# Query and gate projections placed between the convolution blocks of a two-layer hybrid block, with convolution taps read from PSUM

## The chip, the cores and the metric

One core of a Trainium2 chip runs the whole program in one launch. The metric is device time in microseconds, the median of three runs. All times below are microseconds (us) unless marked ns. TensorE is called PE in the rows, VectorE DVE, ScalarE ACT, GpSimd POOL, and SyncE SP, which issues most DMAs.

## What is computed

Two layers of a diffusion backbone over 512 latent tokens (width 1024) and 256 context tokens. The reference, cut to what matters here:

```python
mod = (jax.nn.silu(c) @ mod_w[i] + mod_b[i])           # 6 vectors of 1024, for x and for ctx
h = rms_norm(x, norm_attn_w[i]) * (1.0 + sc_m) + sh_m   # the same for the context
ua, ub, ug = jnp.split(h @ w_in[i], splits, axis=-1)
ya, yca = neighbourhood_attention(ua, uca, na_rpb[i], ctx_out)
yb, ycb = ssd_mixer(ub, ucb, ssd_conv_w[i], ssd_conv_b[i], ...)   # z, xbc, dt; xbc = silu(conv5(xbc))
yg, ycg = gqa_attention(ug, ucg, q_norm_w[i], k_norm_w[i], ctx_out)
x = x + g_m * (jnp.concatenate([ya, yb, yg], axis=-1) @ w_out[i])
x = x + g_f * swiglu(hf, ffn_w_gate[i], ffn_w_up[i], ffn_w_down[i])
```

The second layer gives no context output, so its queries, gates and last two convolution blocks cover 512 tokens and not 768.

## The kernel before, in words

Each fp32 product is made of three fp32r matmuls, from a high and a low half of the weights and of the activations. `load_w` (L321) loads a weight block into one of two raw buffers `wr`, lets ACT write the high half (L326) into one of three buffers `wh`, and DVE subtract to get the low half (L327) into one of three `wl`. `proj_ws` (L338) keeps weights stationary and makes 128 output channels for all tokens in a two-bank PSUM tile `S` (two of them). `proj_as` (L352) keeps 128 tokens stationary and makes 256 or 272 output channels in a one-bank tile, `PT` or `sm` (two of each).

A layer runs: norm 1; query, key and value projections of the neighbourhood attention (`wblk(0)` to `wblk(5)`); `p_kv` (six token blocks, keys, values and dt of the other attention and of the SSD); `p_q` (L711, six token blocks, four in the second layer); eight blocks of `p_xbc` (L749); `p_z` twice (L798, six or four token blocks each); then the attention and SSD units, the output projection, norm 2 and the FFN.

`p_xbc` makes one block of 128 channels: 48 matmuls into `S`; ACT copies the two token ranges into `MA` with zero columns between (L758, L761), after which `S` is free; DVE makes tap 0 and the bias (L763) and taps 1 to 4 (L768) in `MB`; ACT takes the tanh (L772); DVE multiplies (L774, L776); for the first six blocks PE transposes six 128x128 pieces (L785) and ACT copies them out (L791). Beside blocks 0 to 2, `head_out` normalises and rotates key and query heads on POOL (L667, L673) and DVE (L683 to L688); beside blocks 1 to 3 `head_tr` transposes them (L695) and spills them (L282, L283).

The modulation of layer 0 is in twelve chunks of 512 columns. Chunks 0 to 3 are made on PE at the start (`mod_chunk`: eight matmuls at L178, two DVE copies at L185, four small matmuls at L188). Chunks 4 to 9 are made aside by `mod_dots`, each of 16 products on POOL (L228) and 16 sums on ACT (L229) over quarter-megabyte pieces in four `QN` buffers; SP issues those loads (L221) on the same queue as the weight loads (L323). `step_md` calls spread them over the projections and convolution blocks.

The order in each engine's queue is not the order of the text alone. A scheduler goes through all instructions with simulated times, and takes on each engine the first ready one in order of the text, so an engine can be given a later instruction early. The queues that it writes are then run in order on the chip.

Of the kernel before, what the change touches and what calls it, by code (L numbers as in the profile page):

```python
# [28 lines left out]
def hybrid_kernel(ctx: ExitStack, tc: tile.TileContext, a, out, dbg=None):  # L29
# [55 lines left out]
    class Split:  # L85
        """columns 0 .. 511 in one bank of PSUM, the others in another"""
# [12 lines left out]
    WB = {"wr": 2, "wh": 3, "wl": 3}  # L99
# [7 lines left out]
    # ---------------------------------------------------------- constants  # L107
# [42 lines left out]
    # ---------------------------------------------------------- modulation  # L150
# [8 lines left out]
    def mod_loads(l, c, tags):  # L159
        """512 columns of the modulation weights in tiles of the given tags, one or two k per tile"""  # L160
        w, k = [], 0
        for tag in tags:
            if tag in WB:
                wt, n = T(sb, tag, WB[tag], [P, 2, 512]), 2
            else:
                wt, n = T(sb, tag, BUFS[tag], [P, 1, 512]), 1
# [6 lines left out]
    def mod_chunk(l, c, w):  # L173
        """columns 512 c .. 512 c + 511 of the modulation; four row groups of the array take four k"""
# [21 lines left out]
    def mod_rows():  # L196
        """silu of both conditioning vectors as rows on every partition, in four tiles (vector, half)"""
# [11 lines left out]
    def mod_dots(l, c, rows, ptile, aside):  # L209
        """the same columns as mod_chunk by products along rows of the transposed weights"""  # L210
# [50 lines left out]
    # ---------------------------------------------------------- helpers  # L261
# [29 lines left out]
    def spread(rstd, n):  # L291
        """per-token values as a row on every partition"""
# [10 lines left out]
    def make_h(l, xT, h, pbs, part, shi, sc):  # L303
        """norm, scale and shift of one part of the tokens"""
# [16 lines left out]
    def load_w(src, n):  # L321
        raw = T(sb, "wr", 2, [P, n])
        nc.sync.dma_start(raw, src)  # L323
        hi = T(sb, "wh", 3, [P, n], F32R)
        lo = T(sb, "wl", 3, [P, n], F32R)
# [4 lines left out]
    def proj_ws(pt, wh, wl, xh, xl, nk, segs, ks=None):  # L330
        """pt[:, seg] = W^T x, W stationary (nk blocks of 128 rows)"""
# [13 lines left out]
    def proj_as(pt, ws, n, kper, xh, xl, t):  # L345
        """pt[:, :n] = x[t]^T W, activations stationary"""
# [28 lines left out]
    def attn(V2, xk, kts, qcols, bias, yout):  # L375
        """two heads and two blocks of queries; xk: range of x keys (or None); kts: key tiles for P V.
        Returns the steps of the four units: scores and softmax, transposes, and P V where one is complete"""
# [70 lines left out]
    # ---------------------------------------------------------- initial load and transpose  # L448
# [44 lines left out]
    for l in range(L):  # L493
# [9 lines left out]
        # ------------------------------------------------------ norm 1  # L503
# [6 lines left out]
        # ------------------------------------------------------ NA projections  # L510
# [3 lines left out]
        def spill(pt, n, name, scale, perm):  # L514
# [4 lines left out]
            if perm:  # L519
# [564 lines left out]
        for n, _ in enumerate(z for g in range(2) for z in p_z(g)):  # L1084
            if n == 2 * ntt - 2:
                scores(0)
# [284 lines left out]
```

## Time and profile before

| | us |
|---|---|
| runs of the kernel before | 1844.61, 1846.43, 1844.29 (median 1844.61) |
| span of the profiled execution, first to last instruction | 1843.3 |
| PE busy in the span | 1737.0 |
| DVE busy | 1104.0 |
| ACT busy | 681.5 |
| POOL busy | 423.1 |

No separate time is given for the profiled execution; its span is 1.3 below the median of the runs. Busy shares are averages over stages with different limits, so the rows further down are taken by stage: 62.4 to 121.5 (key, value and `p_kv` projections of layer 0), 121.5 to 301.6 (`p_q`, `p_xbc` and `p_z` of layer 0), 301.6 to 475 (its attention units), and 1182.6 to 1291 (`p_q`, `p_xbc` and `p_z` of layer 1). PEclk is the granted clock of TensorE, 1.00 being the upper of its two levels, 2.4 GHz, the lower being 1.2 GHz.

### The profile page before, as it was taken

What the parts mean: (1) busy time and instruction counts of PE and PEld (TensorE: products, weight loads), DVE (VectorE), ACT (ScalarE), POOL (GpSimd) and SP (SyncE); (2) the same over time, 40 slices, a digit from 0 to 9 for tenths busy, and PEclk for the clock granted to TensorE, in tenths of its full rate; (3) what the DMA queues carried; (4) which work ended last, traced back from release to release, by engine and by line L of the source; (5) the groups of instructions that cost most, each with busy time, mean ns of one, the idle gap of its engine ahead of it and who ended that gap; (6) DMA issues with size and microseconds to landing.
All of it is one profiled execution on the core that took longest, in us unless ns stands there. A gap on an engine that the chain in (4) does not pass through costs nothing.

```text
span 1843.3 us, 26677 instructions
## 1 busy us (share of the span) xinstructions
PE 1737.0 (94%) x10146; PEld 1478.4 (80%) x10146; DVE 1104.0 (60%) x2209; ACT 681.5 (37%) x1386; POOL 423.1 (23%) x429
## 2 busy tenths in 40 slices
PE   7987778989999999999999999999899999999998
PEld 3887667777878888888888887989677788888887
DVE  4559996877475555455654576587786743333334
ACT  5554555556344221121112224334555442232222
POOL 0488886654010000000000002241653100000000
PEclk9998889989989999999999999999999999999999
DMA  9542526433123334333443454342631323333332
GB/s 368 201 139 103 163 89 186 140 90 106 56 75 115 114 115 126 103 116 107 124 129 102 130 163 139 96 131 79 183 105 53 108 90 93 99 96 92 103 100 83
DMA packets 94319, 221.66 MB, mean 120 GB/s; under 512 B 18416, under 2 KB 26224, under 8 KB 94192
## 3 DMA queue, kind: packets, MB, share of 16 engines
q1 hardware_dynamic: 78096, 204.65, 35.6%
q10 hardware_dynamic: 16096, 15.31, 2.5%
q8 instruction: 80, 1.31, 0.3%
q14 instruction: 47, 0.39, 0.1%
HBM read 198.49 MB, written 21.43 MB: 119 GB/s over the span
## 4 chain that ended last, share of the span: by engine, by line
PE 76%; DVE 11%; DMA 5%; ACT 3%; issue 2%; POOL 2%; SPq 0%; ACTq 0%; DVEq 0%; POOLq 0%
PE S L338 61%; PE sm L436 3%; DVE MB L768 2%; DMA wl<-crow 2%; PE PT L424 2%; DVE wl L327 1%; PE PT L338 1%; PE PT L352 1%; PE sm L352 1%; DMA wr<-in_mod_wT_dram 1%; DVE wh L892 1%; PE S L390 1%; ACT wh L326 1%; PE sm L913 1%; PE sm L914 1%
## 5 line engine op out<-in xcount | busy, mean ns | idle before, releaser
L326 ACT ACTIVATE wh<-wr 128x1024 fp32r<-128x1024 f32 (+3 forms) x214 | 207.6, 972 | 732.2 <-PE S L338 542.4
L327 DVE TENSOR_TENSOR wl<-wr,wh 128x1024 fp32r<-128x1024 f32 (+3 forms) x214 | 250.0, 1169 | 174.0 <-ACT wh L326 171.6
L269 POOL TENSOR_TENSOR tiny<-tiny,mhalf 128x2 f32<-128x2 f32 (+2 forms) x17 | 28.7, 1688 | 1067.5 <-DVE tiny L1160 1020.3
L338 PE MATMUL S<-HY,wh 128*128 128x512 f32 (+1 forms) x716 | 214.0, 357 | 5.9 <-ACT HY L318 4.1
L338 PE MATMUL S<-HY,wl 128*128 128x512 f32 (+1 forms) x716 | 214.5, 357 | 0.0
L338 PE MATMUL S<-HZ,wh 128*128 128x512 f32 (+1 forms) x716 | 212.8, 355 | 0.8 <-DVE HZ L319 0.8
L338 PE MATMUL S<-HS,wl 128*128 128x512 f32 (+1 forms) x716 | 213.1, 355 | 0.0
L338 PE MATMUL S<-HS,wh 128*128 128x512 f32 (+1 forms) x716 | 211.1, 353 | 0.0
L231 DVE CUSTOM_DVE_ANT_0 PT<-wr,XFB 128x512 f32<-128x512 f32 x112 | 75.5, 715 | 179.8 <-DMA wr<-in_mod_wT_dram 179.8
L338 PEld LDWEIGHTS S<-HY,wh 128*128 128x128 f32 x716 | 119.8, 192 | 27.2 <-ACT HY L318 4.4
L338 PEld LDWEIGHTS S<-HZ,wh 128*128 128x128 f32 x716 | 118.2, 191 | 21.7 <-DVE HZ L319 2.2
L338 PEld LDWEIGHTS S<-HS,wh 128*128 128x128 f32 x716 | 118.8, 191 | 20.2
L338 PEld LDWEIGHTS S<-HY,wl 128*128 128x128 f32 x716 | 118.8, 191 | 18.8
L338 PEld LDWEIGHTS S<-HS,wl 128*128 128x128 f32 x716 | 118.0, 190 | 18.6
L338 PE MATMUL S<-PHA,wh 128*128 128x512 f32 (+1 forms) x358 | 106.4, 355 | 0.0
L338 PE MATMUL S<-PHB,wh 128*128 128x512 f32 (+1 forms) x358 | 105.0, 351 | 0.0
L338 PE MATMUL S<-GX,wh 128*128 128x512 f32 (+1 forms) x400 | 97.2, 349 | 0.4 <-DVE KA L1114 0.4
L415 POOL TENSOR_SCALAR pr<-pr,tiny 128x640 f32<-128x640 f32 (+2 forms) x80 | 69.3, 869 | 84.0 <-DVE tiny L414 64.3
L768 DVE SCALAR_TENSOR_TENSOR MB<-MA,c,MB 128x770 f32<-128x770 f32 (+1 forms) x64 | 85.3, 1333 | 1.4
L228 POOL TENSOR_TENSOR KA<-QN,XFB 128x512 f32<-128x512 f32 x48 | 73.9, 1546 | 44.3 <-ACT XFB L205 23.5
L424 PE MATMUL PT<-c,pr 128*128 128x128 f32 x384 | 66.5, 289 | 13.4 <-POOL pr L415 4.6
L1261 DVE TENSOR_TENSOR MB<-S,MA 128x768 f32<-128x768 f32 (+1 forms) x42 | 34.6, 823 | 72.6 <-PE S L338 72.5
(402 smaller groups left out, 3911.7 us busy)
## 6 DMA issues: line engine op xcount, KB each, us to landing
wr<-in_mod_wT_dram SPq DMA_DIRECT2D x56, 512.0 KB, 3.7
wr<-in_w_gate_dram SPq DMA_DIRECT2D x44, 512.0 KB, 3.5
wr<-in_w_up_dram SPq DMA_DIRECT2D x44, 512.0 KB, 3.5
wr<-in_w_blk_dram SPq DMA_DIRECT2D x28, 512.0 KB, 3.6
wr<-in_w_down_dram SPq DMA_DIRECT2D x32, 448.0 KB, 3.3
QN<-in_mod_wT_dram SPq DMA_DIRECT2D x48, 256.0 KB, 3.3
wr<-in_w_out_dram SPq DMA_DIRECT2D x32, 256.0 KB, 2.6
wr<-in_w_down_dram SPq DMA_DIRECT2D x16, 512.0 KB, 3.4
```

The lines of the kernel that those rows point to most:

```text
L228: G.tensor_tensor(out=p_, in0=wv, in1=x, op=ALU.mult)
L231: V.tensor_tensor_reduce(out=p_, in0=wv, in1=x, scale=1.0, scalar=0.0, op0=ALU.mult, op1=ALU.add, accum_out=acc[:, o : o + 1],)
L269: POW.tensor_tensor(out=y, in0=v, in1=mhalf[:, 0:n], op=ALU.pow)
L326: S.activation(hi, raw, AF.Copy)
L327: V.tensor_tensor(lo, raw, hi.bitcast(F32), ALU.subtract)
L338: ins = PE.matmul(pt[:, c0:c1], lhsT=w, rhs=xx[:, c0:c1], start=(k == (0 if len(order) == 1 else order[0]) and i == 0), stop=(k == (nk - 1 ...
L352: PE.matmul(pt[:, 0:n], lhsT=s, rhs=w[:, o : o + n], start=(k == 0 and i == 0), stop=(k == KB - 1 and i == 2),)
L415: G.tensor_scalar(out=p_, in0=p_, scalar1=m[:, 4:5], scalar2=1.0, op0=ALU.mult, op1=ALU.mult)
L424: PE.transpose(pt[:, k * P : (k + 1) * P], pr[j, qi][:, kk * P : (kk + 1) * P], ident)
L436: PE.matmul(pv[64 * j : 64 * j + 64, 0:P], lhsT=V2(kts[k], j), rhs=ph[j, qi][:, k, :], start=(k == 0), stop=(k == nkt - 1), tile_position= ...
L768: V.scalar_tensor_tensor(ac[:, 0:wid], cp[:, j : j + wid], convw[l][:, b, j : j + 1], ac[:, 0:wid], ALU.mult, ALU.add)
L1261: V.tensor_tensor(gg[:, c0:c1], pu[:, c0:c1], sg[:, c0:c1], ALU.mult)
```

## The change

The token blocks of `p_q` and of both `p_z` are now steps of generators that the loop over the eight convolution blocks calls. In layer 0 two or three token blocks stand behind each block, by the table `fill`; in layer 1 up to three behind five of them. Two token blocks of the second gate set are left to run after the loop, ahead of the attention units. The weights of these sets get buffers of their own, `vh` and `vl`, two of each; the raw buffers `wr` stay two for all.

`p_xbc` no longer copies PSUM out. ACT makes the middle tap and the bias straight from PSUM, DVE makes the other four taps with PSUM as the first input, the tanh is written back to the same PSUM tile, and that tile is free only after the last multiplication. The zero columns between the two token ranges lie in PSUM.

`head_out` and `head_tr` move to later blocks, the key heads get their own inverse root (12 values; 24 for the queries), and `head_tr` uses `PT` and `sm` and spills in two pieces. In layer 0 chunks 4 and 5 of the modulation are made by `mod_chunk` behind the two key projections of the neighbourhood attention, with 16 loads of a quarter megabyte into `GT` buffers; `mod_dots` keeps chunks 6 to 9. The scratch of the descriptors is set to 1024 bytes.

```diff
-    WB = {"wr": 2, "wh": 3, "wl": 3}
+    class Gap:
+        def __init__(self, t):
+            self.t = t
+        def __getitem__(self, idx):
+            c0, c1 = idx[1].start, idx[1].stop
+            o = 0 if c0 < 512 else 4
+            return self.t[:, c0 + o : c1 + o]
+    WB = {"wr": 2, "wh": 3, "wl": 3, "vh": 2, "vl": 2}
...
-    def load_w(src, n):
+    def load_w(src, n, to="w"):
         raw = T(sb, "wr", 2, [P, n])
         nc.sync.dma_start(raw, src)
-        hi = T(sb, "wh", 3, [P, n], F32R)
-        lo = T(sb, "wl", 3, [P, n], F32R)
+        hi, lo = (T(sb, to + p_, WB[to + p_], [P, n], F32R) for p_ in "hl")
...
-                for c in range(4, 10)
+                for c in range(6, 10)
...
             nqk.append(spill(pt, NT, "nk", 1.0, True))
+            if not last:
+                mod_chunk(0, 2 + i, mod_loads(0, 2 + i, (GT[2:10], GT[10:16] + GT[0:2])[i - 2]))
...
-            pt = ps_s()
+            pt = Split()
             for t in range(n // P):
                 PE.transpose(pt[:, t * P : (t + 1) * P], raws[i][:, t, :], ident)
...
-            wq = [load_w(a["w_q"][l, i].rearrange("p k c -> p (k c)"), 1024) for i in range(2)]
+            wq = [load_w(a["w_q"][l, i].rearrange("p k c -> p (k c)"), 1024, "v") for i in range(2)]
             for t in range(ntt):
+                yield
...
-            pt = ps_s()
+            pt = Gap(ps_s())
             proj_ws(pt, w[0], w[1], hh, hl, KB, xsegs if conly else asegs)
-            cp = ma()
-            wid = 512 if conly else 770
...
-            S.activation(cp[:, 2:514], pt[:, 0:512], AF.Copy)
...
+            pt = pt.t
+            wid = 512 if conly else 772
             if not conly:
-                V.memset(cp[:, 772:774], 0.0)
-                S.activation(cp[:, 516:772], pt[:, 512:768], AF.Copy)
+                V.memset(pt[:, 512:516], 0.0)
             ac = mb()
-            V.tensor_scalar(
...
+            S.activation(
+                ac[:, 0:wid], pt[:, 0:wid], AF.Identity, scale=convw[l][:, b, 2:3], bias=convb[l][:, b : b + 1]
             )
-            for j in range(1, 5):
+            for j in (0, 1, 3, 4):
+                s0, s1 = max(0, 2 - j), wid - max(0, j - 2)
                 V.scalar_tensor_tensor(
...
+                    ac[:, s0:s1], pt[:, s0 + j - 2 : s1 + j - 2], convw[l][:, b, j : j + 1], ac[:, s0:s1],
+                    ALU.mult, ALU.add,
                 )
-            th = cp
+            th = pt
...
         p_kv()
-        p_q()
-        r = rsqrt_small(ssr, 36, 1.0 / 64)
+        sets = [p_q(), p_z(0), p_z(1)]
+        fill = [(0, 2), (0, 2), (0, 3), (1, 2), (1, 2), (1, 3), (2, 3), (2, 1)] if not last else (
+            [(0, 2), (0, 3), (1, 0), (1, 2), (1, 3), (2, 0), (2, 2), (2, 0)]
+        )
+        next(sets[0])
+        rk = rsqrt_small(ssr[:, 0:12], 12, 1.0 / 64)
         for b in range(8):
             p_xbc(b)
             step_md(3)
-            if b < 3:
-                head_out(b, qnw[l] if b else knw[l], r, ntok if b else NT)
-            if 1 <= b < 4:
-                head_tr(b - 1, ntok if b > 1 else NT)
+            i, n = fill[b]
+            for _ in range(n):
+                next(sets[i], None)
+            if b < 7 and fill[b + 1][0] > i:
+                next(sets[i + 1])
+                if i == 0:
+                    rq = rsqrt_small(ssr[:, 12:36], 24, 1.0 / 64)
+            for h, b0 in ((0, 0), (1, 3), (2, 4)):
+                nh = ntok if h else NT
+                if b == b0:
+                    head_out(h, qnw[l] if h else knw[l], rq[:, 12 * h - 12 : 12 * h] if h else rk, nh)
+                if b == b0 + 1:
+                    head_tr(h, nh)
...
-        for n, _ in enumerate(z for g in range(2) for z in p_z(g)):
-            if n == 2 * ntt - 2:
+        for n, _ in enumerate(sets[2]):
+            if n == 0:
                 scores(0)
```

## Rows read from the trace of the kernel before

**Rows 1.** The page: the span, and busy time of each engine.
```profile
span 1843.3 us, 26677 instructions
PE 1737.0 (94%) x10146; PEld 1478.4 (80%) x10146; DVE 1104.0 (60%) x2209; ACT 681.5 (37%) x1386; POOL 423.1 (23%) x429
```

**Rows 2.** By stretch: length, busy PE, PEld, DVE, ACT, POOL, granted clock, DMA share, GB/s.
```profile
62.40:121.50 59.10, 55.26 (x344) 49.91 (x342) 22.36 (x46) 35.42 (x90) 39.41 (x36) 0.94 0.56 184
121.50:301.60 180.10, 142.80 (x891) 129.97 (x891) 157.06 (x207) 89.13 (x239) 142.04 (x105) 0.88 0.41 131
...
1182.60:1291.00 108.40, 105.45 (x698) 95.81 (x697) 87.57 (x173) 43.20 (x89) 35.89 (x34) 1.00 0.35 107
```

**Rows 3.** PE's waits from 121.5 to 301.6: total us, times, longest.
```profile
PE PT L785 <- DVE MB L774: 14.0, 3, 9.3
PE PT L785 <- DVE GT L774: 6.9, 2, 4.5
PE PT L352 <- DVE wl L327: 5.4, 1, 5.4
PE S L695 <- DVE GR L686: 4.5, 1, 4.5
```

**Rows 4.** PE's waits from 1182.6 to 1291.
```profile
PE PT L785 <- DVE MB L774: 1.4, 1, 1.4
PE S L338 <- ACT MA L761: 1.1, 1, 1.1
```

**Rows 5.** Timeline of PE: first matmuls of a token block and of two blocks.
```profile
142.88 0.28 PE L352 MATMUL sm<-wh,HY 128*128 128x256 f32 x1
...
145.76 0.51 PE L338 MATMUL S<-HY,wh 128*128 128x512 f32 x2
...
154.25 0.51 PE L338 MATMUL S<-HY,wh 128*128 128x512 f32 x2
```

**Rows 6.** DVE groups from 121.5 to 301.6: count, busy us, mean ns, idle before.
```profile
L768 DVE SCALAR_TENSOR_TENSOR MB<-MA,c,MB 128x770 f32<-128x770 f32 x32 | 51.1, 1597 | 0.7
L327 DVE TENSOR_TENSOR wl<-wr,wh 128x1024 fp32r<-128x1024 f32 x14 | 28.1, 2009 | 4.8 <-ACT wh L326 4.8
...
L763 DVE TENSOR_SCALAR MB<-MA,c 128x770 f32<-128x770 f32 x8 | 9.6, 1195 | 0.0
L776 DVE SCALAR_TENSOR_TENSOR MB<-MA,MB 128x256 f32<-128x256 f32 x4 | 4.9, 1227 | 0.0
...
L283 DVE TENSOR_TENSOR pr<-S,pr 128x768 fp32r<-128x768 f32 x3 | 2.8, 949 | 1.1 <-ACT pr L282 1.1
L806 DVE SCALAR_TENSOR_TENSOR SA<-SA,PT 128x256 f32<-128x256 f32 x6 | 2.5, 416 | 2.7 <-ACT SA L805 2.6
```

**Rows 7.** Timeline of DVE around 120: the longest single subtraction.
```profile
120.40 6.42 DVE L327 TENSOR_TENSOR wl<-wr,wh 128x1024 fp32r<-128x1024 f32 x1 [0.99 <-ACT wh L326]
```

**Rows 8.** DVE groups from 1200 to 1290 (layer 1).
```profile
L768 DVE SCALAR_TENSOR_TENSOR MB<-MA,c,MB 128x770 f32<-128x770 f32 x24 | 27.7, 1156 | 0.5
L327 DVE TENSOR_TENSOR wl<-wr,wh 128x1024 fp32r<-128x1024 f32 x9 | 11.3, 1251 | 6.1 <-ACT wh L326 5.9
```

**Rows 9.** Timeline of PE: a modulation chunk, its first and its last matmuls.
```profile
26.39 0.62 PE L178 MATMUL S<-wh,cs 128*32 128x512 f32 x2
...
30.75 1.05 PE L188 MATMUL S<-c,SA 128*128 128x2 f32 x8 [0.30 <-DVE SA L185]
```

**Rows 10.** POOL and ACT groups of the modulation's products, 60 to 301.
```profile
L228 POOL TENSOR_TENSOR KA<-QN,XFB 128x512 f32<-128x512 f32 x48 | 73.9, 1546 | 44.3 <-ACT XFB L205 23.5 <-DMA QN<-in_mod_wT_dram 17.0 <-ACT KA L229 3.6
...
L229 ACT ACTIVATE QN<-QN 128x512 f32<-128x512 f32 x48 | 30.1, 627 | 12.3 <-POOL QN L228 7.3 <-POOL KA L228 2.4 <-DVE SA L806 2.3
```

**Rows 11.** ACT groups of the weights' high halves and of the tanh, 60 to 301.
```profile
L326 ACT ACTIVATE wh<-wr 128x1024 fp32r<-128x1024 f32 x17 | 17.9, 1053 | 11.6 <-PE S L338 7.0 <-DMA wr<-in_w_blk_dram 4.2 <-issue 0.2
...
L772 ACT ACTIVATE MA<-MB 128x770 f32<-128x770 f32 x8 | 6.8, 846 | 34.3 <-DVE MB L768 34.3
```

**Rows 12.** Weight loads from 121.5 to 301.6: count, KB each, us to landing.
```profile
wr<-in_w_blk_dram SPq DMA_DIRECT2D x8, 512.0 KB, 3.5
```

More of the change, by code (lines that the diff above doesn't have):

```diff
@@ L162, in mod_loads @@
         for tag in tags:
-            if tag in WB:
+            if tag in ("wh", "wl"):
                 wt, n = T(sb, tag, WB[tag], [P, 2, 512]), 2
@@ L518, in spill @@
                 hi, lo = (T(sb, "pr", 3, [P, NT], F32R) for _ in range(2))
-            if perm:
-                pr_ = [(0, 512)] + ([(512, n)] if n > 512 else [])
-            else:
-                pr_ = [(0, n)]
-            for c0, c1 in pr_:
+            for c0, c1 in [(0, 512)] + ([(512, n)] if n > 512 else []):
                 sv, hv, lv = pt[:, c0:c1], hi[:, c0:c1], lo[:, c0:c1]
@@ L684, in head_out @@
             V.tensor_tensor(c, c, s, ALU.add)
-            rb = r[:, 12 * i : 12 * i + 12].rearrange("p (t h) -> p t h", h=2).unsqueeze(3)
+            rb = r.rearrange("p (t h) -> p t h", h=2).unsqueeze(3)
             V.tensor_tensor(v4(raw[:, 0:4, :]), v4(c), rb[:, 0:4].to_broadcast([P, 4, 2, 64]), ALU.mult)
@@ L717, in p_q @@
                     head_in(pt[:, i * P : (i + 1) * P], 1 + i, t)
-                step_md(1)
+            yield
         def gqa_sets():
@@ L775, in p_xbc @@
             if not conly:
-                V.scalar_tensor_tensor(o[:, 512:768], th[:, 514:770], 1.0, ac[:, 514:770], ALU.add, ALU.mult)
+                V.scalar_tensor_tensor(o[:, 512:768], th[:, 516:772], 1.0, ac[:, 516:772], ALU.add, ALU.mult)
             if b < 6:
@@ L798, in p_z @@
         def p_z(g):
-            wz = [load_w(a["w_z"][l, g, i].rearrange("p k c -> p (k c)"), 1024) for i in range(2)]
+            wz = [load_w(a["w_z"][l, g, i].rearrange("p k c -> p (k c)"), 1024, "v") for i in range(2)]
             for t in range(ntt):
@@ L807, in p_z @@
                 nc.scalar.dma_start(zsp[g][:, t, :], th)
+            yield
         p_kv()
-        p_q()
-        r = rsqrt_small(ssr, 36, 1.0 / 64)
+        sets = [p_q(), p_z(0), p_z(1)]
[4 more added lines that the diff above has]
+        rk = rsqrt_small(ssr[:, 0:12], 12, 1.0 / 64)
         for b in range(8):
@@ L1082, in events @@
                 ev.pop(0)[2]()
-        for n, _ in enumerate(z for g in range(2) for z in p_z(g)):
-            if n == 2 * ntt - 2:
+        for n, _ in enumerate(sets[2]):
+            if n == 0:
                 scores(0)
-            if n == 2 * ntt - 1:
+            if n == 1:
                 scores(1)
@@ L1295, in _layout @@
     r["ctx"] = g["ctx"][0]
-    r["mod_w"] = c(g["mod_w"][0, :, 0:2048])
+    r["mod_w"] = c(g["mod_w"][0, :, 0:3072])
     r["mod_wT"] = c(g["mod_w"].transpose(0, 2, 1)).reshape(2, 48, 128, 1024)
@@ L1360 @@
     arrs = _layout(inputs)
-    nc = _bacc.Bacc("TRN2", target_bir_lowering=False, num_devices=1)
+    nc = _bacc.Bacc("TRN2", target_bir_lowering=False, num_devices=1, dynamic_dma_scratch_size=1024)
     arrays, aps = {}, {}
```

5 lines of the change are left out of this document (removed).

## The prediction

> **What bounds the kernel now.** I read the page first. PE is busy for 1737.0 of 1843.3 us [rows 1], so a gain can come only where PE waits or runs at a low clock, or where its work gets less. I then cut the span into stretches. In layer 0 the queries, convolution blocks and gates take 180.1 us, with 37.3 us in which PE is idle and a granted clock of 0.88, while DVE is busy for 157.06 us; in layer 1 the same work, less the context's part, takes 108.4 us with PE busy for 105.45 at a clock of 1.00 [rows 2]. So almost the whole loss lies in layer 0. PE's waits there say what ends last: transposes wait for the convolution's last steps on DVE (14.0 and 6.9 us), token blocks for a weight's low half (5.4), head transposes for the scaled heads (4.5) [rows 3]. All of these are DVE. In layer 1 the two longest waits are 1.4 and 1.1 us [rows 4].
>
> DVE is slow in layer 0 because of what runs beside it. A tap with both inputs in SBUF takes 1597 ns [rows 6] against 1156 in layer 1 [rows 8]; POOL is busy for 142.04 of 180.1 us in the one and 35.89 of 108.4 in the other [rows 2]. The gate's last multiplication with both inputs in SBUF takes 1227 ns for 256 columns, and one of the same size with an input in PSUM takes 416 in the same stretch [rows 6]. Once a subtraction of two SBUF tiles took 6.42 us [rows 7]. So operations with two SBUF inputs lose time beside POOL and those with an input in PSUM don't.
>
> **What PE needs at the least.** A token block takes 145.76 − 142.88 = 2.88 us and a convolution block 154.25 − 145.76 = 8.49 us, both at the upper clock [rows 5]. Layer 0 has what layer 1 has (105.45) plus two query and four gate token blocks (6 × 2.88 = 17.3) plus 256 more columns in two blocks (2 × 8.49 / 3 = 5.7): 128.4 us. The room in layer 0 is 180.1 − 128.4 = 51.7 us, in layer 1 108.4 − 105.45 = 3 us.
>
> **The change, part by part.** *Taps.* The 32 taps of layer 0 read PSUM. The nearest row is an operation of 768 columns with one input in PSUM, 949 ns in the same stretch [rows 6]; I take 0.95. DVE saves 32 × (1.597 − 0.95) = 20.7 us. Tap 0 goes to ACT, which saves DVE 9.6 [rows 6] and replaces two copies on ACT by one pass, about even; ACT is busy for 89.13 of 180.1 [rows 2], which covers it. The last two multiplications now read the tanh from PSUM: for the four 256-column ones that the rows show, 4 × (1.227 − 0.416) = 3.2, and for all sixteen I take 6. Two of six modulation chunks go from POOL, an estimated 3 us of small DVE work here. DVE's 157.06 becomes about 118. The bounds of a tap are 0.95 and the 1.156 of layer 1 [rows 8], which would give back 6.6 us.
>
> The Trainium skill speaks against this part ("VectorE: DVE Perf Modes", Rules for kernel authors): it advises to copy PSUM to SBUF first where many operations follow, and its cycle table charges 62 cycles more for a PSUM source, an estimate of 65 ns or 4.2 us over 64 taps. By it the sum would come out at most 4.2 us later; the rows above, beside a busy POOL, point the other way, and I follow them.
>
> *Interleaving.* With DVE at 118 against PE's floor of 128.4, PE should set the pace, as in layer 1, where DVE is busy for 87.57 of 108.4 us, 81% [rows 2]. But layer 0 would stand at 92%, and the order is fixed by simulated times while POOL's interference is real, so some waits stay. POOL loses 32 of 96 products of 1546 ns and ACT 32 sums of 627 ns [rows 10]; neither was what PE waited for, so I count nothing beyond the interference, where the bound is the low halves: 14 × (2.009 − 1.251) = 10.6 us of DVE [rows 6, 8]. I put the loss in layer 0 at 18.7 us: 6 at two handovers (below), 7 of other waits, 5.7 of slow clock (before, 51.7 − 37.3 = 14.4 beside 37.3 of idling, the same proportion). Bounds: 3, as in layer 1, and 35, if DVE's order still makes PE wait. Gain 33 us, between 16 and 48.
>
> *Handovers.* The sets have only two `vh` and two `vl`, both in use until a set's last token block. Then ACT (1.05 us [rows 11]) and DVE (2.0 [rows 6]) must split the next weights: about 3 us until PE can go on with the next token block, two per layer. In layer 1 one of the two stands ahead of a block with no tokens behind it and is covered: 3 us there, against the 2.5 of waits that go [rows 4]. With `S` held through a convolution, a block's conv (two passes of ACT like the tanh's 0.85 [rows 11], four taps of 0.95, and about 1.1 for the last multiplications: 6.6 us) must end before PE is through the next block (8.49): covered, unless DVE is late by 2 us where no token block follows. I take +1 for layer 1, between −3 and +12.
>
> *Modulation on PE.* A chunk occupies PE from 26.39 to 31.8, 5.4 us with some transposes of other work between [rows 9]; I take 4 us each, 8 in all, in a stretch of 59.1 us where PE idles for only 3.84 [rows 2]. Nothing hides them beyond that: +4 if they fall into the idle time, +15 if PE also waits for the two copies on DVE, or for 4 MB more in a stretch with DMA already at 0.56 [rows 2], queued on SP ahead of the weights. The products removed there are loads of the same size that came later. I take +8.
>
> *Start of the attention units.* Twelve token blocks (35 us) used to stand between the last convolution and the units in layer 0, eight (23) in layer 1; two remain. What they hid, the decays' round trip through DRAM and the first loads, may now be late: 0 to 9 us per layer; I take +1 each. The other edits (inverse roots, later `head_tr`, the scratch) lie beside this and I count nothing for them; if POOL's inverse root for the keys comes late, `head_tr` makes PE wait at most as long as now, 4.5 [rows 3].
>
> **Sum.** 1843.3 − 33 + 8 + 1 + 2 = 1821.3 in the profiled execution's span; the median of the runs stands 1.3 above that span, so 1822.6, say 1823. Own range 1810 to 1838.
>
> **The rivals.** *PE takes over fully.* Layer 0 ends with layer 1's loss of 3 us (−48.7), the modulation costs 4: about 1800. For it: all of PE's long waits are on work that shrinks. Against it: low halves with two SBUF inputs and a POOL that is still busy. *DVE still paces.* Only 17 of the 51.7 us come back: 1843.3 − 17 + 8 + 3 + 1.3 = 1839, from 1832 to 1846. For it: DVE's 118 plus weights of 6.42 us now and then [rows 7] in a shorter stretch with the same POOL work per us. Against it: DVE was idle for 23 us of the stretch as well. *The order hardly changes.* The scheduler takes what is ready whatever the text says, so the queues may come out much as before, and only DVE's saving acts: about 1838. Against it: token blocks wait for weights that the text loads last.
>
> *Slower: weights queue behind weights.* The raw buffers `wr` are two for all sets. A new set's two weights wait in them for `vh`, so the next block's weights cannot be loaded until those are split: 1.05 + 2.0 [rows 11, 6], then a load of 3.5 [rows 12], then 1.05 + 2.0 again, 9.6 us per handover. If the planned order puts that block first, PE stands still, and the clock adds two fifths (14.4 / 37.3): 13 us, four times, 53 in place of the 9 counted and not covered. 1822.6 + 53 − 9 = 1867. It decides the sign from about 7 us per handover on. Against it: the scheduler takes the first ready instruction, and the new token block is ready sooner than the block.
>
> **How the numbers follow.** Forecast 0.52, PE takes over fully 0.13, DVE still paces 0.18, order hardly changes 0.05, weights queue 0.12. What a measurement can tell from no change here is about 0.2%, 3.7 us, so faster means below 1840.9 and slower above 1848.3. Faster: 0.50 + 0.13 + 0.11 + 0.03 = 0.77. The same: 0.01 + 0.06 + 0.01 + 0.01 = 0.09. Slower: 0.12 + 0.02 from the edges of the others = 0.14. The range that leaves out the slower rival and about half of the full gain goes from 1803 to 1846.
>
> **What would show it.** The tap row in layer 0 should read near 950 ns; the stretch from the first query token block to the first scores of layer 0 near 147 us at a clock above 0.94, with DVE near 118 busy; no wait of L785 over 4 us. The stretch from 62 to its end should be longer by some 8 us with L178 and L188 in it. Waits of L352 or L338 for L327 of 3 us at the handovers are in the sum; waits of 9 or more there, or a layer 1 stretch above 115, would make the forecast wrong, and so would taps above 1.2 us.

## The result, and the profile after

The changed kernel takes **1862.5 us** (median of 5 runs, 1858.8 to 1871.4) against 1844.6 before (5 runs, 1842.7 to 1847.5): 1.0094 of the time, 95% interval 1.0065 to 1.0122. It is slower, where 1823 was forecast. Its profiled execution was its slowest, 1871.4 with a span of 1869.6; a second profile, below, had 1860.0.

The page of the changed kernel, the lines that answer to [rows 1]:

```profile
span 1869.6 us, 26595 instructions
...
PE 1753.0 (94%) x10194; PEld 1489.6 (80%) x10194; DVE 1058.0 (57%) x2175; ACT 665.0 (36%) x1312; POOL 350.5 (19%) x399
```

DVE and POOL lost 46 and 73 us of work, as planned, and the span grew all the same: busy time that falls on an engine that isn't waited for is worth nothing, and PE, which is, got 16 us busier (the two chunks' matmuls are about 7 of it). By stretches, in the columns of [rows 2] (norm 1 and the projections up to the last key and value token; layer 0 up to its last gate token; its attention; layer 1 from its last key and value token to its last gate token):

```profile
62.40:143.50 81.10, 65.77 (x395) 56.16 (x396) 39.70 (x51) 42.41 (x109) 53.99 (x46) 0.89 0.52 167
143.50:299.90 156.40, 135.43 (x891) 123.76 (x889) 101.22 (x180) 60.92 (x145) 63.06 (x66) 0.93 0.35 109
299.90:474.70 174.80, 153.41 (x1117) 123.28 (x1115) 128.90 (x365) 102.72 (x287) 92.77 (x121) 0.93 0.38 114
1188.50:1309.90 121.40, 109.17 (x694) 98.95 (x693) 72.46 (x145) 39.26 (x71) 30.29 (x34) 0.96 0.25 81
```

Layer 0 went from 180 to 156.4 us, not to 147. The stretch ahead of it grew by 22 us, not 8, and layer 1 from 108.4 to 121.4, with PE idle for 12.2 us where it had been idle for 3. DVE is at 101 of 156.4 in layer 0: it no longer sets the pace, yet PE still waits for it there (columns of [rows 3]):

```profile
PE PT L791 <- DVE MB L780: 13.3, 2, 7.3
PE PT L791 <- DVE GT L780: 3.3, 1, 3.3
PE S L348 <- ACT wh L336: 1.7, 2, 1.3
```

and in layer 1 it waits for a weight (columns of [rows 4]):

```profile
PE S L348 <- ACT wh L336: 5.1, 1, 5.1
PE sm L362 <- ACT SA L661: 2.4, 1, 2.4
PE PT L791 <- DVE GT L780: 2.4, 1, 2.4
```

The names behind the arrows don't tell why. The loads do. SP's timeline in layer 1 of the changed kernel, from just after its last key and value token: the two gate weights go into the two raw buffers, and no weight follows for 30 us.

```profile
1189.39 1.74 SPq L334 DMA_DIRECT2D wr<-in_w_z_dram  x2
1220.63 0.33 SPq L605 DMA_DIRECT2D GR<-in_rpb_dram  x1
1221.06 0.37 SPq L334 DMA_DIRECT2D wr<-in_w_blk_dram  x1
1221.49 0.42 SPq L605 DMA_DIRECT2D GR<-in_rpb_dram  x1
1223.14 0.33 SPq L334 DMA_DIRECT2D wr<-in_w_blk_dram  x1
```

ACT's timeline there says why: the gate weights can be split only when the queries' token blocks have freed `vh`, and that is at 1218.57.

```profile
1218.57 1.06 ACT L336 ACTIVATE vh<-wr 128x1024 fp32r<-128x1024 f32 x1 [1.21 <-PE PT L362]
...
1220.63 1.08 ACT L336 ACTIVATE vh<-wr 128x1024 fp32r<-128x1024 f32 x1
```

For 29 us both raw buffers hold weights that nobody can use yet, and the next convolution block's weights can't be fetched. At the second change of sets it is the same (loaded from 1231, split from 1267), and then PE stands for 5.05 us. In layer 0 no weight load is issued between 153.6 and 208.6; the first gate weight, loaded at 151.1, is split at 205.7. SP's timeline there:

```profile
153.59 0.37 SPq L334 DMA_DIRECT2D wr<-in_w_z_dram  x1
154.38 32.53 SPq L232 DMA_DIRECT2D QN<-in_mod_wT_dram  x9
...
208.55 7.69 SPq L334 DMA_DIRECT2D wr<-in_w_blk_dram  x3
```

SP's queue itself comes free at nearly the same times. In layer 1 it stands in front of a bias load that waits for head transposes until 1220.63 and 1269.52, and the first raw buffer is free at 1220.89 and 1269.39; in layer 0 attention loads go out until 208.46, and the buffer is free at 207.99. In the changed kernel either alone would have held the block's weights back about as long. Experiment e9, on top of e5, takes the queue's part away.

The program's order fits that. These are PE's matmuls in layer 1 in the order in which they ran, `t` those of token blocks (24 each), `B` those of convolution blocks (48 each) and `h` head transposes, other work left out; the second line is the kernel of experiment e5:

```
changed: t15 B4 t8 B44 t1 B48 t16 t32 t24 h6 t29 B4 t2 B92 t16 B48 t1 t24 t24 h4 t13 t11 B72 t24 B20 h4 t24 B4 t24
e5:      t15 B4 t8 B44 t1 B48 t16 t8 B14 t24 B11 B10 B2 h2 B6 t24 h4 B5 t48 B48 B48 B25 t24 B19 B4 t24 h4 t13 t11 B24 t1 B2 t2 B18 h4 t24 B4 t1 t44
```

The changed kernel runs four token blocks in a row and then two convolution blocks, where its text for layer 1 never has more than two token blocks between two convolution blocks (the threes in `fill` include a step that makes none). The text interleaves them, and the weights don't let it happen: in e5 only the order of the loads differs, and PE's order comes out another.

### The profile page after: what moved, and what is told of

The parts are those of the page before. It is cut to its first block, busy times and chain, and to the rows that moved or that the text cites. A ratio compares the mean times of both kernels' runs of the same rounds, so it can differ in the third digit from the quotient of the medians.

```text
span 1869.6 us, 26595 instructions
## 1 busy us (share of the span) xinstructions
PE 1753.0 (94%) x10194; PEld 1489.6 (80%) x10194; DVE 1058.0 (57%) x2175; ACT 665.0 (36%) x1312; POOL 350.5 (19%) x399
## 4 chain that ended last, share of the span: by engine, by line
PE 78%; DVE 9%; DMA 7%; ACT 3%; issue 2%; POOL 1%; SPq 0%; ACTq 0%; DVEq 0%; POOLq 0%
PE S L348 60%; PE PT L362 3%; PE sm L446 3%; DMA wl<-crow 2%; PE sm L362 2%; DMA wr<-in_mod_wT_dram 2%; PE PT L434 1%; PE PT L348 1%; DVE wl L337 1%; PE S L400 1%; DMA wr<-in_w_blk_dram 1%; PE sm L934 1%; PE S L189 1%; PE sm L935 1%; DVE wh L913 1%
## 5 line engine op out<-in xcount | busy, mean ns | idle before, releaser
L336 ACT ACTIVATE wh<-wr 128x1024 fp32r<-128x1024 f32 (+4 forms) x202 | 194.9, 967 | 729.6 <-PE S L348 517.6
L337 DVE TENSOR_TENSOR wl<-wr,wh 128x1024 fp32r<-128x1024 f32 (+4 forms) x202 | 235.2, 1165 | 191.4 <-ACT wh L336 189.5
L280 POOL TENSOR_TENSOR tiny<-tiny,mhalf 128x2 f32<-128x2 f32 (+3 forms) x19 | 26.8, 1412 | 1068.2 <-DVE tiny L1181 1024.3
L348 PE MATMUL S<-PHA,wh 128*128 128x512 f32 (+1 forms) x358 | 104.8, 351 | 0.0
L348 PEld LDWEIGHTS S<-GX,wh 128*128 128x128 f32 x400 | 66.3, 190 | 11.6 <-DVE KA L1135 0.8
L773 DVE SCALAR_TENSOR_TENSOR MB<-S,c,MB 128x770 f32<-128x770 f32 (+3 forms) x64 | 63.0, 985 | 15.3 <-ACT MB L768 14.0
```

The source lines that it names most:

```text
L280: POW.tensor_tensor(out=y, in0=v, in1=mhalf[:, 0:n], op=ALU.pow)
L336: S.activation(hi, raw, AF.Copy)
L337: V.tensor_tensor(lo, raw, hi.bitcast(F32), ALU.subtract)
L348: ins = PE.matmul(pt[:, c0:c1], lhsT=w, rhs=xx[:, c0:c1], start=(k == (0 if len(order) == 1 else order[0]) and i == 0), stop=(k == (nk - 1 ...
L773: V.scalar_tensor_tensor(ac[:, s0:s1], pt[:, s0 + j - 2 : s1 + j - 2], convw[l][:, b, j : j + 1], ac[:, s0:s1], ALU.mult, ALU.add,)
```

## The experiments

Each kernel is timed beside the kernel before on its own chip: e1 to e4 on one chip, e5 to e8 on a second, e9 to e15 on a third. Between these groups medians of the same program can differ: e5 has 1830.5 (1829.4 to 1835.9) and e13, the same program, 1840.0. The table gives the median, its ratio to before (95% interval), and from the one profile of each the length of four stretches: from the start to layer 0's last key and value token (early), from there to its last gate token (layer 0), from there to the end of its attention, and layer 1 from last key and value token to last gate token.

| kernel | median | ratio | early | layer 0 | attention 0 | layer 1 |
|---|---|---|---|---|---|---|
| before | 1844.6 | | 120.9 | 180.5 | 168.0 | 108.4 |
| changed | 1862.5 | 1.0065 to 1.0122 | 143.5 | 156.4 | 174.8 | 121.4 |
| e1 taps alone | 1834.4 | 0.9932 to 0.9964 | 123.5 | 160.2 | 167.1 | 108.3 |
| e2 taps and chunks on PE | 1831.1 | 0.9899 to 0.995 | 141.5 | 144.9 | 162.0 | 109.1 |
| e3 taps and order | 1902.9 | 1.028 to 1.0346 | 122.2 | 210.4 | 170.2 | 119.0 |
| e4 = e3, weights ahead | 1882.4 | 1.0182 to 1.0235 | 125.9 | 198.1 | 176.6 | 113.6 |
| e5 = changed, weights ahead | 1830.5 | 0.9912 to 0.9948 | 133.1 | 144.8 | 167.7 | 114.7 |
| e6 order in layer 0 only | 1843.7 | 0.9981 to 1.0006 | 135.9 | 156.6 | 171.0 | 110.8 |
| e7 order in layer 1 only | 1836.3 | 0.9942 to 0.9981 | 130.1 | 148.9 | 161.9 | 120.3 |
| e8 = e3, later key heads | 1855.0 | 1.0038 to 1.0082 | 122.4 | 178.1 | 166.6 | 116.7 |
| e9 = e5, bias loads on ACT | 1841.7 | 0.9979 to 1.0011 | 142.4 | 144.4 | 170.9 | 114.4 |
| e10 = e5, product loads on ACT | 1847.1 | 1.0002 to 1.0045 | 146.3 | 144.7 | 170.9 | 117.7 |
| e11 = e5, no products | 1826.4 | 0.988 to 0.9929 | 136.5 | 134.6 | 170.6 | 117.3 |
| e12 changed, again | 1861.8 | one run | 140.6 | 156.8 | 170.3 | 120.2 |
| e13 = e5, again | 1840.0 | one run | 141.5 | 143.2 | 174.3 | 113.2 |
| e14 = e5, late products | 1851.3 | 1.0014 to 1.0048 | 129.4 | 156.8 | 172.0 | 115.1 |
| e15 = e2, late products in the text alone | 1835.3 | 0.9927 to 0.9963 | 134.8 | 150.4 | 162.4 | 110.5 |

**Part by part (e1 to e4).** e1 is the kernel before with the new `p_xbc`, `Gap` and `head_tr`; e2 adds the two chunks; e3 is the changed kernel without them (`range(4, 10)` for the products again):

```diff
-                for c in range(6, 10)
+                for c in range(4, 10)
...
-            if not last:
-                mod_chunk(0, 2 + i, mod_loads(0, 2 + i, (GT[2:10], GT[10:16] + GT[0:2])[i - 2]))
```

> The kernel before with the new taps alone (taps from PSUM, head transposes in PT and sm); no interleaving, no chunk moved. Theory T (the loss is made by the chunks on PE in the first stretch and by the interleaving's weight queue): the taps alone are faster, 1844 minus 15 to 30, so 1815 to 1830, with layer 1's stretch from query blocks to scores near 108 us. Rival R (the S tile held through the convolution makes PE wait): layer 1's stretch 115 us or more, and the total at 1840 or above.

> The new taps and the two modulation chunks on PE, in the old order of projections. Theory T: 15 to 25 us slower than the taps alone, all of it before 146 us (last key and value token block 15 to 23 us later). Rival R (the early loss is PE's 8 us of chunk work, the rest comes from interleaving): 5 to 10 us slower than the taps alone.

> The changed kernel without the two chunks on PE (chunks 4 to 9 aside, as before); taps and interleaving stay. Theory T: 15 to 25 us faster than the changed kernel, so 1838 to 1847, with layer 1's stretch still 15 us longer than before. Rival R: 5 to 10 us faster than the changed kernel, 1853 to 1857.

The taps alone take 11 us off, the chunks another 3, and both without the new order make the best of the four: e2 is faster than either kernel. The new order costs 31 us with the chunks (1831.1 to 1862.5) and 68 without (1834.4 to 1902.9). So it is the order that costs, and the chunks, which cost 18 us early (123.5 to 141.5), give 15 of it back in layer 0, where POOL has a third fewer products beside DVE. Neither theory had expected this: theory T had the early 18 us right, but e2 came out 3 us faster than e1, not 15 to 25 slower, and e3 40 us slower than the changed kernel, not faster. That a tile held through the convolution makes PE wait (rival R) is refuted by e1, whose layer 1 stretch is 108.3 as before.

**Weights ahead (e4, e5).** The next block's weights are loaded before the next set's two:

```diff
-        def p_xbc(b):
+        def p_xbc(b, w):
             conly = last and b >= 6
-            w = wblk(6 + b)
...
+        wx = [wblk(6)]
...
-            p_xbc(b)
+            p_xbc(b, wx[b])
+            if b < 7:
+                wx.append(wblk(7 + b))
```

> As the run without the chunks, but the next convolution block's weights are loaded ahead of the next set's, so that they do not queue behind weights that wait for vh and vl. Theory T (weights queue behind weights): 8 to 20 us faster than the run without the chunks, layer 1's stretch 105 to 113 us instead of 120. Rival Q (the loads of the attention bias ahead on SP, which wait for the head transposes, hold the weights back): within 3 us of the run without the chunks, layer 1's stretch still 117 or more.

> The changed kernel, with the next block's weights loaded ahead of the next set's two. If the weights queueing behind weights in the two raw buffers are the main loss (theory T), the waits of S for a weight's high half (6.3 us over layer 0, 5.1 in layer 1) and of the token blocks for low halves (7.3 in layer 0) go, the layer 1 stretch from the last key and value token to the last gate token falls from 121.4 to about 112, and the median comes down by some 20 us, as it did without the modulation move (1902.9 to 1882.4): 1842. If the queue of SP is held by the neighbourhood bias loads, which wait for a buffer that PE's head transposes free (theory Q: 49.7 us of such waits in layer 1), the same loads stand behind the same held queue and layer 1 stays above 118; the median falls by 5 us at most, to 1857 or more.

On e3 it takes 20.5 us off, 9 of them from a wait for the key heads (53.2 to 44.1 us, see e8). On the changed kernel it takes off **32**: in these runs that one is as fast as e2. The layer 0 stretch is back at 144.8, and layer 1 is at 114.7, below the 118 that the rival theory gave it; the median fell far beyond that theory's 5 us, and by more than the 20 us expected (see e12 and e13). SP's timeline of e5 in layer 1 shows the edit at work: a block's weights go in first, ahead of the gate weights and of the bias loads, and although the gate weights then hold both buffers just as long, PE has that block to run meanwhile.

```profile
1159.46 0.33 SPq L334 DMA_DIRECT2D wr<-in_w_blk_dram  x1
1160.87 5.08 SPq L334 DMA_DIRECT2D wr<-in_w_z_dram  x2
1196.60 0.80 SPq L605 DMA_DIRECT2D GR<-in_rpb_dram  x2
1197.50 2.13 SPq L334 DMA_DIRECT2D wr<-in_w_blk_dram  x2
```

**One layer at a time (e6, e7).** The old order, with `p_q` ahead of the blocks and `p_z` behind them, where `il` is false:

```diff
+        il = not last          # e7: il = last
...
-        sets = [p_q(), p_z(0), p_z(1)]
+        if il:
+            sets = [p_q(), p_z(0), p_z(1)]
...
+        else:
+            for _ in p_q():
+                step_md(1)
...
```

> Taps from PSUM and the chunks on TensorE in both layers, the new order in layer 0 alone; layer 1 in the order of before. The kernel without the new order took 1831.1, with it 1862.5. By the stretches of the two profiles layer 0 gives 11.5 of the loss up to its last gate token and 12.8 more in the attention that follows, layer 1 12.3. If both layers lose by the same mechanism and the losses add, this kernel takes 1831 + 20 to 26 = 1851 to 1857 and its layer 1 stretch is 109. If layer 0's loss is only clock and run to run spread of the profiled execution (the profiled one was 9 us above its median), it takes about 1840.

> The same with the new order in layer 1 alone. If the losses add: 1831 + 12 = 1843, layer 1 stretch about 121, layer 0 stretch 145. There is no modulation work and little POOL work beside layer 1 (30.3 of 121.4 us busy), so a loss here can only be the order itself: weights behind weights (T) or the held queue (Q). If it comes out at 1831, layer 1's loss was carried over from layer 0.

The stretches add as expected: with the order, layer 0 has 156.6 (e2: 144.9) and layer 1 has 120.3 (e2: 109.1), as in the changed kernel. The medians are below what was expected, 12.6 and 5.2 above e2 where the whole order costs 31.4: the early stretch, whose text is the same, came out 6 and 11 us shorter, on another chip than e2's. With that added back they are 18 and 17 above e2. It is taken up with e12.

**The key heads (e3 and e8).** The 68 us of e3 have one wait in them. PE's longest wait of e3 in layer 0, and POOL's timeline where it ends:

```profile
PE PT L701 <- DVE GR L692: 53.2, 1, 53.2
```

```profile
213.24 1.28 POOL L239 TENSOR_TENSOR QN<-QN,YO 128x512 f32<-128x512 f32 x1
214.47 2.27 POOL L280 TENSOR_TENSOR tiny<-tiny,mhalf 128x12 f32<-128x12 f32 x1
216.70 1.27 POOL L239 TENSOR_TENSOR KA<-QN,XFB 128x512 f32<-128x512 f32 x1
```

`head_tr(0)` stands early in PE's order. It needs the scaled keys, these need the keys' inverse root, and that 2.27 us operation stands on POOL behind products that run one after the other from 185 on. Everything behind the transposes in PE's queue waits along. e8 moves these transposes two blocks later:

```diff
-                if b == b0 + 1:
+                if b == b0 + (3 if h == 0 else 1):
                     head_tr(h, nh)
```

> The new order without the modulation move, as the run that took 1902.9, with the key heads' transposes two blocks later in the text. There PE waited once for 53.2 us, in front of these transposes, for the scaled key heads; POOL began the keys' inverse root only at 214.5 us, behind modulation products that ran one after the other from 185 on. If the early place in PE's order made that wait (theory H), it shrinks to under 15 us and the median falls by 30 to 50, to 1855 to 1873, near the kernel with the modulation move (1862.5): the 40 us that the move is worth under the new order are then this wait. If the wait only moves to other work (POOL holds something else that PE needs), the median stays above 1890.

The wait shrinks to 9.0 us and the median falls by 48, so the early place in PE's queue made it. In the changed kernel it doesn't occur: POOL has a third fewer products, and the root runs at 171.2. So the 40 us that the chunks seemed to be worth under the new order were this wait; with it mostly gone, the kernel without them (e8, 1855.0) is 7 us faster than the changed one.

**The queues (e9, e10).** DMAs moved from SP to ACT, each in e5: the neighbourhood bias loads, or those of the products.

```diff
-                nc.sync.dma_start(t2[:, i], rp[:, r0 : r0 + 48, :])
+                nc.scalar.dma_start(t2[:, i], rp[:, r0 : r0 + 48, :])
```

```diff
-                    nc.sync.dma_start(wv, src[:, hs_])
+                    nc.scalar.dma_start(wv, src[:, hs_])
```

> The kernel of the weights loaded ahead (1830.5), with the neighbourhood bias loads issued on ACT's queue in place of SP's. In its layer 1, SP's queue stands for 64.7 us in all (29.0 the longest) in front of these loads, which wait for PE's head transposes; behind them stand block weights. If the held queue (theory Q) is what keeps its layer 1 stretch at 114.7 us against 109.1 without the new order, the stretch falls to about 110 and the median by 4 to 8 us, to about 1824. If the weights themselves are the limit (two raw buffers), or PE's floor, nothing changes within 3 us. It could also lose, if ACT stands still in front of the same wait: then ACT's work in that stretch starts later and the median rises.

> The kernel of the weights loaded ahead (1830.5), with the loads of the modulation products issued on ACT's queue, which makes their buffers free, in place of SP's, which waits for them (27.2 us in ten waits between 130 and 450 us) with weights behind. If SP's order holds weights back in layer 0, the early stretch (62 to 133.1 us here) and layer 0 (144.8 us) come down by some 5 us together, to 1825. [...]

Neither helps. e9's layer 1 stretch is 114.4 against 114.7, so the bias loads at the head of SP's queue, for all their 64.7 us, held up nothing that PE waited for: with them gone, the second block's weights are issued 38.6 us after the last key and value token (39.0 in e5), since the raw buffers are full until then (the first is free at 1207.92, the load goes out at 1207.95). So the buffers alone are enough to hold the weights back. Both medians are above e5's, by 11 and 17 us, but e5's program took 1840.0 on their chip (e13, one run), and against that they are 2 and 7 above. Their early stretches are 142.4 and 146.3, e13's is 141.5. What the loads cost on ACT is not shown.

**What POOL does to DVE (e11 to e15).** The early stretch is 133.1 in e5 and 143.5 in the changed kernel, though their text differs little there. One instruction makes 6.1 of these 10.4 us. DVE's timeline of the changed kernel at 89, and of e5 at the same place:

```profile
88.99 7.93 DVE L337 TENSOR_TENSOR wl<-wr,wh 128x816 fp32r<-128x816 f32 x1 [5.04 <-ACT wh L336]
```

```profile
89.34 1.80 DVE L337 TENSOR_TENSOR wl<-wr,wh 128x816 fp32r<-128x816 f32 x1 [5.01 <-ACT wh L336]
```

In the first, POOL ran six products without a break beside it, and the subtraction ended 0.87 us after the last of them (96.05). In the second, one product gave way, the only one of 2.08 us among others of 1.3. POOL's timeline of each:

```profile
94.78 1.27 POOL L239 TENSOR_TENSOR KA<-QN,XFB 128x512 f32<-128x512 f32 x1
```

```profile
90.22 2.08 POOL L239 TENSOR_TENSOR QN<-QN,HD 128x512 f32<-128x512 f32 x1
```

e12 and e13 are the two kernels unchanged, e11 leaves the 64 products out (the modulation values of four chunks are then other ones), e14 and e15 take out the calls that begin them ahead of the convolution blocks and in `p_kv`:

```diff
-                        G.tensor_tensor(out=p_, in0=wv, in1=x, op=ALU.mult)
-                        S.activation(p_, p_, AF.Copy, accum_out=acc[:, o : o + 1])
+                        S.activation(wv, wv, AF.Copy, accum_out=acc[:, o : o + 1])
```

```diff
-            step_md(4)             # twice, ahead of the blocks of keys and values
...
-                step_md(1)         # in p_kv
```

> The changed kernel once more, for its profile. In its first profile the subtraction of 816 columns at 89.0 us took 7.93 us beside POOL's products and the last key and value token came at 143.5 us; the profile with the weights loaded ahead had 1.80 us there and 133.1. If the long one is chance, one of the repeated profiles of the two kernels shows the other value; if it belongs to the program, this one has it again at the same place, and the 10 us of the early stretch belong to the difference between the two kernels.

> The kernel of the weights loaded ahead once more, for its profile. If the long subtraction belongs to the program, it is 1.80 us again near 89 us and the last key and value token comes near 133 us; if it is chance, it may be 7.9 us, with that token near 142.

> The kernel of the weights loaded ahead with the 64 modulation products of POOL left out; the loads and ACT's sums stay, so the modulation values of four chunks are other ones. It measures what POOL's row of products costs the others. If DVE's subtractions of two SBUF tiles are held up by POOL (in one profile the same subtraction of 816 columns took 7.93 us until POOL's products ended, in another 1.80 beside the same products), no low half in layer 0 takes over 1.8 us, their mean falls from 1.34 us to about 1.2, the taps with their one SBUF source stay at 0.95 to 1.02, and the median falls by 5 to 12 us, to 1818 to 1825, with runs closer together. If the long ones come from transfers, which stay, they are still there.

> The kernel of the weights loaded ahead (1830.5), with POOL's modulation products, and their loads on SP, begun only beside the convolution blocks, so that the early stretch has neither. If POOL's products are what makes DVE late there, its subtractions all take under 1.8 us before 130 us, the last key and value token comes at 126 to 130 us in place of 133.1 to 143.5, whatever the run, and the median falls by 3 to 8 us, to 1822 to 1827; layer 0 gives back some 2 us, as the products now share it with the convolution, whose taps read PSUM. If the early stretch is bound by its loads, it stays above 132 and the median within 3 us; if the products get too long for layer 0, the taps and low halves there are slower and it is 1835 or more.

> The same for the kernel with the order of before (taps from PSUM and chunks on TensorE, 1831.1): products begun beside the convolution blocks. If POOL's products are what makes DVE late early on, the last key and value token comes at 126 to 130 us in place of 141.5 and the median falls by 5 to 10 us, to 1821 to 1826. With both orders at the same time the new order is worth nothing; if this one is more than 3 us faster than the other, the new order costs even with its weights loaded ahead.

It is not the program alone. e13, the same kernel as e5, had the long one, and its key and value tokens ended at 141.5:

```profile
90.87 7.85 DVE L337 TENSOR_TENSOR wl<-wr,wh 128x816 fp32r<-128x816 f32 x1 [5.14 <-ACT wh L336]
```

e12, the changed kernel again, took 1.80 us for that subtraction and 8.11 for the next, at 104.8. That it is chance is not fully shown: e5 and e13 ran on different chips. On e5's chip, e5, e6 and e7 had no subtraction over 4 us and e8 one of 7.73, at 123.0; on e13's, e9, e10, e12, e13 and e15 had one each, though not always the same one. So it isn't the chip alone either, but a part of the chip's isn't ruled out. Without products (e11, on e13's chip) no DVE operation of the whole run took over 4 us (one low half still took 2.56), and layer 0 went at a clock of 0.99:

```profile
136.50:271.10 134.60, 129.14 (x891) 119.43 (x890) 83.83 (x169) 43.40 (x87) 30.61 (x38) 0.99 0.29 92
```

Its layer 0 stretch is 10 us shorter; its median is 4 below e5's, where the two intervals overlap, and 14 below e13's one run on its own chip. Beginning the products later shortens the early stretch to 129.4 in the new order, where only 4 of the 64 products then run and no low half takes over 1.23 us, and loses it again: in e14 layer 0 takes 156.8, PE waits 8.1 us for the key heads once more, and one rotation of heads on DVE took 11.50 us at 180.6. Against e13, on its chip, e14 is 11 us slower.

e15 doesn't test this in the old order. The calls in `p_q` stay there, POOL begins the products at 78.0, and 36 of the 64 run ahead of the last key and value token, as many as in e2. So e15 is e2 over again on another chip, at 1835.3 against 1831.1, and what late products do in the old order is not shown. On that chip the old order (1835.3, 1830.2 to 1839.4) and the new with its weights ahead (e13, 1840.0, one run) lie 5 us apart.

With like compared with like (e12 and e13, one chip, a long subtraction early in both) the weights' edit is worth 13.6 us in layer 0 and 7.0 in layer 1; these two runs differ by 21.8 us. Their stretches, e12 first:

```profile
140.60:297.40 156.80, 135.41 (x890) 123.89 (x889) 100.24 (x183) 62.85 (x148) 64.67 (x67) 0.93 0.34 109
1179.90:1300.10 120.20, 109.61 (x695) 98.89 (x694) 72.45 (x145) 39.41 (x71) 30.42 (x34) 0.96 0.26 83
```

```profile
141.50:284.70 143.20, 131.35 (x891) 121.39 (x890) 102.86 (x183) 63.29 (x148) 65.13 (x67) 0.95 0.39 120
1171.10:1284.30 113.20, 107.35 (x695) 96.55 (x694) 74.25 (x149) 40.51 (x74) 29.85 (x36) 0.97 0.29 89
```

The 32 us between the medians hold some of what the early stretch does, chance or chip, as well.

## Why the prediction was wrong

By stretches the changed kernel's profile differs from the one before by +22.6 us early, −24.1 in layer 0, +6.8 in its attention, +13.0 in layer 1, +6.5 in the attention after it and +1.5 elsewhere: 26.3 in all, where −22 was forecast.

**The step that failed: interleaving, a gain of 33, and the handovers, 3 us each.** The mechanism of the weights' rival, given 0.12 and 1867 us, is what happened (1862.5). The forecast priced a change of sets as the two splits of a weight. The rival's text had the mechanism, two raw buffers for all sets, with the block's load behind the set's, and argued it away: the scheduler would run the token block that is ready first. It did, and then ran all token blocks of the set before it had a convolution block's weights. A buffer's price is how long it is held, and this one is held not for the 9.6 us of loads and splits but for 29 in layer 1 and 55 in layer 0, until the set before has ended. That the rival's 1867 lies so near is in part luck: it kept the gain of 33 and added 44 us at the handovers, where the order of the loads was worth 20.6 in the two stretches (e12 to e13) and the interleaving gained nothing.

**Where the 33 us went.** The stretch of layer 0 came down by 35.6 us with no new order at all (180.5 to 144.9 in e2): 20.3 from the taps, 15.3 from the chunks. The forecast had seen that DVE beside POOL made PE wait [rows 2, 3], and then booked the whole relief to the interleaving. With DVE relieved there was little left for an order to win: e2's PE idles for 10.2 us in layer 0 and 3.9 in layer 1.

```profile
141.50:286.40 144.90, 134.69 (x894) 124.38 (x893) 107.38 (x189) 69.17 (x161) 68.17 (x69) 0.95 0.41 126
1159.80:1268.90 109.10, 105.18 (x698) 95.74 (x697) 79.18 (x155) 43.76 (x82) 29.21 (x34) 1.00 0.35 107
```

With its weights ahead the new order gives 144.8 and 114.7 there: nothing in layer 0, 5.6 us worse in layer 1.

**Layer 1, +1 forecast.** +13.0, above the 12 of its bound and past the 115 named as the mark of error. It is layer 0's loss again (11.2 us over e2 in e7), with no modulation work beside it. The weights' edit gives back 6.7 to 7.0 of it; what makes the rest is not shown.

**Taps: right.** 0.95 us forecast, 1.02 measured. DVE's groups in layer 0 of the changed kernel, which answer to [rows 6]:

```profile
L773 DVE SCALAR_TENSOR_TENSOR MB<-S,c,MB 128x771 f32<-128x771 f32 x16 | 16.3, 1019 | 0.4
...
L337 DVE TENSOR_TENSOR wl<-wr,wh 128x1024 fp32r<-128x1024 f32 x8 | 10.4, 1305 | 12.5 <-ACT wh L336 12.5
...
L812 DVE SCALAR_TENSOR_TENSOR SA<-SA,PT 128x256 f32<-128x256 f32 x6 | 2.5, 417 | 1.6 <-ACT SA L811 1.6
```

A tap from PSUM takes the same without POOL's products (1018 ns in e11). From SBUF it took 1597 ns beside them and 1156 away from them on average [rows 6, 8]; 18 of those 24 in layer 1 took 1.01 to 1.02 us, as from PSUM, and six were held up. The advice of the Trainium skill to copy PSUM to SBUF first where many operations follow ("VectorE: DVE Perf Modes", Rules for kernel authors) doesn't pay here: no tap was faster from the copy, and on average they were slower, in layer 1 too. The 62 cycles that the prediction took from that page's table don't show: the fastest taps take 1007 ns from either memory. The Trainium skill's page "SBUF — State Buffer" (Who interferes with whom) says that a VectorE instruction with two SBUF inputs contends with a GpSimd instruction that reads SBUF and that one with at most one such input, outside the two-port modes, doesn't; these rows agree. DVE in layer 0 came to 101 us, not 118.

**Modulation, +8 forecast, 4 to 15.** It cost 18 early (e1 to e2) and gave 15 back in layer 0, which the forecast had counted as nothing beyond the low halves. The two chunks keep PE for 7 us; the rest is waits for weights. The third block's load is issued on SP at 53.6 in e2, behind the chunks' loads, and at 45.4 in e1; ACT splits it only at 65.4, behind its copies and stores of the block before, and PE waits 4.6 us for that. Another 6.2 us are a wait for a long subtraction, which e5 to e7 didn't have: their early stretches are 7 to 12 us above e1's, close to the 8 forecast. That the chunks are the loss falls with e2.

**Key heads, at most 4.5 us.** True of the changed kernel (no wait at all), and only by luck: the forecast looked at how long the wait was, not at what stands on POOL ahead of the root. With the 96 products of before in place of 64 it was 53.2 us (e3).

**Attention start, +1 each: too small, the cause open.** In layer 0 it goes with the order. With the chunks, attention takes 161.9 to 162.4 us in the three profiles with the old order there (e2, e7, e15) and 167.7 to 174.8 in the nine with the new, weights ahead or not: 5 to 13 us that the weights' edit doesn't give back. PE idles for 16.1 to 16.9 us of it in the one group and for 17.4 to 23.9 in the other; the rest is work at a lower granted clock (0.98 against 0.92 to 0.97). At the start the changed kernel's PE waited 3.0 and 3.9 us for a scores tile that the softmax was still reading, but before it was 6.2 in one wait, so that isn't it. No run separates the order's share from the clock's. In layer 1 the attention's 6.5 us are not the order's: 135.2 in the changed kernel, 134.9 in e2.

## What to carry to other kernels

Before work is interleaved, ask of each buffer that both kinds share how long the one kind holds it, from load to last use, and put the loads of the work that can run next ahead of the loads of the work that must wait. Apply the other parts of a change alone first: what relieves the bound may leave nothing for the order to gain. An instruction that is moved early in an in-order queue is safe only if all that feeds it is early in its own queues.

## What was not expected of the hardware

A DVE operation with two SBUF inputs can be held far beyond one POOL instruction: 7.9 us in place of 1.8 for a 816-column subtraction, over six products in a row that each ran at their full speed; 8.10 and 7.32 us for operations on 8 and 12 columns (e3 at 167.0 and 216.8); 11.50 in e14. With POOL's products left out none took over 4 us (e11). The Trainium skill ("SBUF — State Buffer", SBUF: two separate sides) describes the ports that VectorE and GpSimd share as a lock that one instruction holds while the other blocks; that the one which waits can lose it again to the next instruction and the next is more than it states, and is inferred here from the timelines. It comes in one execution of a program and not in another, and whether by chance or by the chip is open. The two profiles of one kernel have their early stretch end at 133.1 and 141.5, with about 6 of these 8 us in one subtraction: reason enough to take a second profile, on the same chip, before a difference of that size is explained by an edit.
